# Queries and keys turned by two transposing DMAs instead of six TensorE transposes and two copies

## The chip, the cores and the metric

The kernel runs on one NeuronCore of a Trainium2 chip. Its engines each work through a list of instructions in order: TensorE (PE in the profile, with PEld for the loading of the stationary operand), VectorE (DVE), ScalarE (ACT), GpSimd (POOL) and SyncE (SP), which here issues all DMAs. The metric is the device time of one execution in microseconds; lower is better.

## The reference

One inference step of a single hybrid layer, for 1024 frames of a new stream and 32 frames of a running one (1056 rows, model width 1024). Cut to what matters here:

```python
z = rmsnorm(x, g) @ w_in                      # q,k,v of attention; q,k,v,gate of retention; two gates
qa = rmsnorm(qa.reshape(B, T, 8, 2, 64), g_q) # 8 heads, two maps of 64 each
ka = rmsnorm(ka.reshape(B, T, 8, 2, 64), g_k)
s  = einsum('bqhcd,bkhcd->bhcqk', qa, ka) * 64**-0.5    # chunk-causal mask, chunks of 64
p  = softmax(s);  a = p[:, :, 0] - lam * p[:, :, 1]
o_a = diff_out(einsum('bhqk,bkhe->bqhe', a, va))
o_r = ret_out(retention(qr, kr, vr), g_ret)   # chunkwise-recurrent, with decay
x = x + (sigmoid(gate_a) * o_a + sigmoid(gate_r) * o_r) @ w_o
x = x + (silu(h @ w_gate) * (h @ w_up)) @ w_down
x = x + sigmoid(rmsnorm(x) @ w_ple_gate) * (p_in @ w_ple)
```

The normalised keys and the values are outputs as well, as is the retention state.

## The kernel before

Inputs are float32. Each matmul operand is held as a float16 pair, high and low part, and a product is three float16 matmuls. The first part of the kernel, up to about 1040 us, does the projections, attention and retention; the second part does the output projection, the feed-forward block and the last gate. Only the first part is touched by the change.

The first part works on 72 units, (head h, tile i) for 8 heads and 9 tiles. Tiles i = 0 to 7 are 128 rows of the new stream; tile i = 8 is the 32 rows of the running stream, which is worked on as 128 partitions with 32 valid rows (R = 128, RT = 32). For each step, `project` makes one PSUM bank `pj` (128 x 512) for the A side of unit s (query, key, value, retention query and key; lines 734 to 736, or 745 for i = 8) and one for the B side of unit s - 4 (retention value and gates). Then:

- `unit_a` scales query and key into `z` (L1022), normalises them (L1036 to L1045), stores the key and the value as output (`kv`, L1048 on POOL and the DMA L1049), makes the float16 pairs of query and key in the tile `qst` (six groups of 128 columns: two for the query, four for the key; L1060 and L1061 on ACT, L1063 and L1064 on DVE), and turns them: six TensorE transposes (L1072) into one PSUM bank of the pool "o", then two copies through the helper at L388, one into `kT` (four groups, at the columns of this tile) and one into `q4` (two groups).
- `attend` computes scores from `q4` and `kT` (L875, L878; L877 adds the mask), the maxima (L885), the exponentials (L895), combines both maps (L909), turns the result (L924, L931 to L935), and multiplies by the values (L943 to L947).
- `unit_b` does the retention (L1142 to L1175), the gates, and the mix, which is turned (L1237) and stored to DRAM by a DMA (`mixT`, L1246).

`kT` has one buffer for a head (all tiles), `q4` and `qst` have two, `mixT` four; three PSUM banks serve the pool "o", one pair of banks the scores.

The order of the instructions on PE, DVE, ACT and POOL is written out by a planner, the class `Flow`, when the program is built. Each unit is a generator that yields what it needs: `M(us)` for PE, `V(n)` for DVE, `S(n)` for ACT, `G(n)` for POOL, `DM(mb)` for DMA (a resource "D"), `either(...)` for a choice, ("get", pool) and ("put", pool) for a buffer, ("wait", event), and ("delay", us). The planner starts whatever can start earliest by these costs (`LAT` = 0.13 us between dependent steps on different engines, `MARGIN` = 0.3 us ahead of a step of PE that follows another engine's), and the instruction is emitted at that moment. On the chip each engine then runs its list in order and waits where an input is not there yet. The DMAs on SP are not in the hand-written order of these four engines; they are queued in SP's own list. The loads of weights are L407, 1 MB each, for blocks that are used later.

Of the kernel before, what the change touches and what calls it, by code (L numbers as in the profile page):

```python
# [12 lines left out]
F16 = mybir.dt.float16  # L13
# [8 lines left out]
P = 128  # L22
D = 1024
# [35 lines left out]
def V(n, f=1.0, x=0.0):  # L59
    return {"V": 0.07 + x + f * n / 960.0}  # L60


def S(n, x=0.0):
    return {"S": 0.1 + x + n / 1200.0}


def G(n, x=0.0):
    return {"G": 0.15 + x + 0.0021 * n}


def M(us):
    return {"M": us}


def DM(mb):
    return {"D": mb * 2.9}


def either(*ds):
    out = {}  # L80
    for d in ds:
        out.update(d)
    return out
# [100 lines left out]
def kernel(  # L184
# [26 lines left out]
    nc = tc.nc  # L211
# [11 lines left out]
    def sm(n, tag, bufs=2, dt=F32):  # L223
        return small.tile([P, n], dt, tag=tag, name=tag, bufs=bufs)
# [162 lines left out]
    def copy(e, out, in_):  # L387
        (nc.scalar.copy if e == "S" else ENG[e].tensor_copy)(out, in_)  # L388
# [99 lines left out]
    with ExitStack() as pa:  # L488
# [3 lines left out]
        id16 = ca.tile([P, P], F16, name="id16")  # L492
# [24 lines left out]
        ps_o = pa.enter_context(DT(name="ps_o", bufs=3, space=PSUM))  # L517

        cs_sb = hp.tile([P, NT, 2, 32], F32, name="cs_sb")
        kT = hp.tile([P, 4, T], F16, name="kT")  # L520
# [227 lines left out]
        def fold(i, ps):  # L748

            if i < NT - 1:  # L750
                return ps, "pj"
            yield ("get", "su")
            yield S(P)
            su = wk.tile([P, 4, TS], F32, tag="su", name="su", bufs=1)
            psv = ps[:, 0:8 * TS].rearrange("p (g a c) -> p g a c", g=4, a=2)
            nc.scalar.copy(su, psv[:, :, 1])
            yield V(P)
            nc.vector.tensor_tensor(out=suz[:, :, 0:TS], in0=psv[:, :, 0], in1=su, op=ALU.add)
            yield M(0.5)
            for g in range(4):  # L760
                nc.tensor.transpose(out=ps[:, g * P:g * P + P], in_=suz[:, g], identity=id32)
            yield ("put", "su")
            return ps, "pj"

        def rms_small(ss, R, n, tag):

            yield G(0, 0.5 + 0.2 * n)
            r = sm(n, tag + "r", 6)
            nc.gpsimd.tensor_scalar(out=ss[0:R], in0=ss[0:R], scalar1=EPS, scalar2=None, op0=ALU.add)
            nc.gpsimd.tensor_tensor(out=r[0:R], in0=ss[0:R], in1=neghalf[0:R, 0:n], op=ALU.pow)  # L770
            return r
# [239 lines left out]
        def unit_a(h, i, ps, dA, e):  # L1011
            R, RT = P, P if i < NT - 1 else TS
            t0 = i * P
            yield ("wait", ("pa", h))
            if i == NT - 1:
                yield ("wait", ("cache", h))
            yield ("prio", -1)
            ps, buf = yield from fold(i, ps)
            yield ("get", "z")
            yield S(256, 0.05)  # L1020
            z = wk.tile([P, 2, P], F32, tag="z", name="z", bufs=3)
            nc.scalar.activation(z[0:R], ps[0:R, 0:256], AF.Copy, scale=dA[0][0:R])  # L1022
            yield ("get", "kv")
            kv = wk.tile([P, 2, P], F32, tag="kv", name="kv", bufs=3)
            if h * NT + i >= NQ:
                yield ("wait", ("ret",) + divmod(h * NT + i - NQ, NT))
            yield ("get", "rot")
            zr = wk.tile([P, P], F32, tag="zr", name="zr")
            flow.add(values(h, i, R, ps, kv, zr, dA, e, buf, (h, i)), 1)
            yield ("prio", 0)  # L1030

            zg = z.rearrange("p a (b c) -> p (a b) c", b=2)
            yield ("get", "sqz")
            yield S(256)
            sq = wk.tile([P, 4, 64], F32, tag="sqz", name="sqz")
            nc.scalar.activation(sq[0:R], zg[0:R], AF.Square, scale=0.125)  # L1036
            yield V(256)
            ss = sm(4, "qss", 6)
            nc.vector.tensor_reduce(out=ss[0:R], in_=sq[0:R], axis=AX.X, op=ALU.add)
            yield ("put", "sqz")  # L1040
            r = yield from rms_small(ss, R, 4, "qk")
            g = yield either(G(256), V(256))
            ENG[g].tensor_tensor(out=zg[0:R], in0=zg[0:R], in1=r[0:R].unsqueeze(2).broadcast_to([R, 4, 64]), op=ALU.mult)
            g = yield either(G(256), V(256))
            ENG[g].tensor_tensor(out=z[0:R], in0=z[0:R], in1=gqk[0:R], op=ALU.mult)  # L1045
            yield ("wait", ("v", h, i))
            yield G(128)
            nc.gpsimd.tensor_tensor(out=kv[0:R, 0], in0=z[0:R, 1], in1=kun[0:R].broadcast_to([R, P]), op=ALU.mult)  # L1048
            nc.sync.dma_start(out=kvo[h, t0:t0 + RT], in_=kv[0:RT])  # L1049
            yield ("later", ("kv", 3.0))  # L1050
            if i == NT - 1:
                yield V(P, 0.5)
                nc.vector.tensor_scalar(out=z[0:R, 1], in0=z[0:R, 1], scalar1=e["kre"][0:R], scalar2=None, op0=ALU.mult)

            yield ("get", "qst")
            yield S(384, 0.1)
            st = wk.tile([P, 6, 2, 64], F16, tag="qst", name="qst")
            zqk = z[0:R].rearrange("p a (m c) -> p a m c", m=2)
            sf = st[0:R].rearrange("p g a c -> p (g a) c")
            nc.scalar.copy(sf[:, 0:4:3], zqk[:, 0])  # L1060
            nc.scalar.copy(st[0:R, 2:4], zqk[:, 1].unsqueeze(2).broadcast_to([R, 2, 2, 64]))  # L1061
            yield V(384, 1.0, 0.07)
            nc.vector.tensor_tensor(out=sf[:, 1:3], in0=zqk[:, 0], in1=sf[:, 0:4:3], op=ALU.subtract)  # L1063
            nc.vector.tensor_tensor(out=st[0:R, 4:6], in0=zqk[:, 1].unsqueeze(2).broadcast_to([R, 2, 2, 64]),  # L1064
                                    in1=st[0:R, 2:4], op=ALU.subtract)
            yield ("put", "z")
            yield ("get", "o")
            yield M(0.336)
            pt = ps_o.tile([P, 1024], F16, tag="o", name="t")
            ptv = pt[:, 0:768].rearrange("p (g c) -> p g c", g=6)  # L1070
            for g in range(6):
                nc.tensor.transpose(out=ptv[:, g, 0:R], in_=st[0:R, g].rearrange("p a c -> p (a c)"), identity=id16[0:R, 0:R])  # L1072
            yield ("put", "qst")
            if h and i < NT - 1:
                yield ("wait", ("s", h - 1, NT - 2))
            g = yield either(V(512, 0.5), S(512, -0.09))
            copy(g, kT[:, :, t0:t0 + RT], ptv[:, 2:6, 0:RT])
            yield ("get", "q4")
            g = yield either(V(256, 0.5), S(256, -0.07))
            q4 = wk.tile([P, 2, P], F16, tag="q4", name="q4")  # L1080
            copy(g, q4[:, :, 0:R], ptv[:, 0:2, 0:R])
            yield ("put", "o")
            if i < NT - 1:

                if i:
                    yield ("wait", ("k", h, i - 1))
                yield ("set", ("k", h, i))
                NK = t0 + P
                sblocks = [(b0, min(512, NK - b0), kT[:, :, b0:min(b0 + 512, NK)]) for b0 in range(0, NK, 512)]
                yield from attend((h, i), i, R, q4, sblocks, True, [(P, vh[:, j, 0], vh[:, j, 1]) for j in range(i + 1)],  # L1090
                                  NK, scs, e["do_p"])
            else:
                sblocks = [(0, PAST, e["kcs"]), (PAST, TS, kT[:, :, t0:t0 + TS])]
                vblocks = [(P, e["vcs"][:, j, 0], e["vcs"][:, j, 1]) for j in range(4)]
                vblocks.append((P, vh[:, i, 0], vh[:, i, 1]))
                yield from attend((h, i), i, R, q4, sblocks, False, vblocks, PAST + TS, e["sc"], e["do_s"])
            yield ("put", "A")
            yield ("set", ("oa", h, i))
# [271 lines left out]
        def stream():  # L1370
# [10 lines left out]
            for s in range(NT * H + LAG):  # L1381
                at[0] = s
                h, i = divmod(s, NT)
                if h < H:
# [29 lines left out]
                    yield from project(wAs[h][0], ps, i, s)  # L1414
                    yield ("set", ("pA", s + 1))
                    flow.add(unit_a(h, i, ps, wAs[h][1], env[h]), 0)
                    if i == NT - 1:
                        yield ("put", "w")
# [670 lines left out]
```

## Time and profile before

| | |
|---|---|
| time, median of 3 runs | 1910.07 us (1909.86 to 1910.68) |
| span of the profiled execution | 1908.6 us |
| PE busy | 1859.8 us (97%) |
| DVE busy | 1497.7 us (78%) |
| ACT busy | 1087.3 us (57%) |
| POOL busy | 680.9 us (36%) |
| DMA | 146.90 MB, mean 77 GB/s |

The span is from the first to the last instruction of one execution under the profiler; nothing else of that execution is listed. An engine's busy time is the time in which at least one of its instructions runs. Matmuls overlap each other, so their listed durations add up to more than PE's busy time. In lists of groups, the middle number of three is the median duration in ns, and "xN" the number of instructions. A row "A <- B: t, n, m" in a list of waits says that A was idle for t us in total, n times, at most m us at once, until B ended. SPq is the queue of DMA issues on SP: the listed length is that of the issue, not of the transfer.

### The profile page before, as it was taken

How to read it: one execution, taken by the hardware profiler on the slowest of the kernel's cores; microseconds unless marked ns; L12 is line 12 of the kernel's file. 1: busy time of each engine (PE TensorE's matmuls, PEld its weight loads, DVE VectorE, ACT ScalarE, POOL GpSimd, SP SyncE). 2: the span in 40 equal slices, each digit the busy share in tenths (PEclk: the TensorE clock that was granted, in tenths of full speed). 3: DMA queues.
4: the chain of work that ended last, by engine and by line, in shares of the span. 5: the costliest groups of instructions: out<-in, count | busy, mean ns of one | idle time of the engine just before them, and what ended most of it. 6: DMA issues, size and time to landing. Idle time of an engine off the chain costs nothing.

```text
span 1908.6 us, 38365 instructions
## 1 busy us (share of the span) xinstructions
PE 1859.8 (97%) x14223; PEld 1220.3 (64%) x14223; DVE 1497.7 (78%) x3940; ACT 1087.3 (57%) x2842; POOL 680.9 (36%) x1149
## 2 busy tenths in 40 slices
PE   7999999999999999999999997999999999999999
PEld 3556565555655566655556685777777776666666
DVE  7888888788787787777887589999999986654364
ACT  7777677677676776766666345655555552101132
POOL 3654444445444544544442067333232300000010
PEclk9999999999999999999999999999999999999999
DMA  5222112112021121211215610222211116112031
GB/s 194 70 72 78 60 32 82 36 55 83 24 70 58 50 64 34 79 59 31 85 33 187 226 65 31 101 86 83 69 55 66 47 54 262 61 62 79 10 133 50
DMA packets 71949, 146.90 MB, mean 77 GB/s; under 512 B 25265, under 2 KB 52145, under 8 KB 63826
## 3 DMA queue, kind: packets, MB, share of 16 engines
q1 hardware_dynamic: 71762, 144.46, 22.7%
q8 instruction: 111, 1.82, 0.4%
q14 instruction: 76, 0.62, 0.1%
HBM read 113.09 MB, written 31.34 MB: 76 GB/s over the span
## 4 chain that ended last, share of the span: by engine, by line
PE 73%; DVE 12%; POOL 7%; ACT 5%; issue 2%; DMA 1%; SPq 0%; POOLq 0%; ACTq 0%; DVEq 0%
PE ps L474 10%; PE ps L475 10%; PE ps L476 10%; PE pj L734 7%; PE pj L736 7%; PE pj L735 7%; PE ps L1478 4%; PE ps L1477 4%; PE ps L1476 4%; ACT p L895 2%; DVE nm L885 2%; DVE w L467 1%; POOL qkr L770 1%; PE sc L875 1%; PE sc L878 1%
## 5 line engine op out<-in xcount | busy, mean ns | idle before, releaser
L734 PE MATMUL pj<-w,xh 128*128 128x512 f16 x1024 | 389.0, 380 | 2.8 <-ACT w L465 2.8
L735 PE MATMUL pj<-w,xh 128*128 128x512 f16 x1024 | 389.0, 380 | 0.6 <-DVE w L467 0.6
L736 PE MATMUL pj<-w,xh 128*128 128x512 f16 x1024 | 389.0, 380 | 0.0
L475 PE MATMUL ps<-mixs,w 128*128 128x352 f16 (+1 forms) x960 | 260.4, 276 | 5.9 <-DVE mixs L1501 5.9
L474 PE MATMUL ps<-mixs,w 128*128 128x352 f16 (+1 forms) x960 | 260.4, 276 | 0.3 <-ACT pws L1354 0.3
L476 PE MATMUL ps<-mixs,w 128*128 128x352 f16 (+1 forms) x960 | 260.5, 276 | 0.0
L476 PEld LDWEIGHTS <-w 128*128 128x128 f16 x1736 | 170.4, 98 | 56.2 <-issue 6.0
L474 PEld LDWEIGHTS <-w 128*128 128x128 f16 x1736 | 170.6, 98 | 54.4 <-issue 4.4
L475 PEld LDWEIGHTS <-w 128*128 128x128 f16 x1736 | 170.4, 98 | 49.8 <-issue 1.6
L736 PEld LDWEIGHTS <-xh 128*128 128x128 f16 x1024 | 100.3, 98 | 122.3 <-issue 1.9
L1634 POOL TENSOR_TENSOR st<-st 128x512 f32<-128x512 f32 x66 | 88.2, 1336 | 244.7 <-DVE w L1629 186.6
L734 PEld LDWEIGHTS <-xh 128*128 128x128 f16 x1024 | 101.3, 99 | 76.7 <-issue 3.7
L735 PEld LDWEIGHTS <-xh 128*128 128x128 f16 x1024 | 100.2, 98 | 74.6 <-issue 3.7
L895 ACT ACTIVATE p<-sc,nb,scs 128x256 f32<-128x256 f32 (+7 forms) x128 | 106.4, 832 | 71.5 <-POOL nb L887 49.0
L474 PE MATMUL ps<-tT,w 128*128 128x352 f16 (+1 forms) x528 | 144.0, 277 | 0.0
L475 PE MATMUL ps<-tT,w 128*128 128x352 f16 (+1 forms) x528 | 143.9, 277 | 0.0
L476 PE MATMUL ps<-tT,w 128*128 128x352 f16 (+1 forms) x528 | 143.8, 277 | 0.0
L1629 DVE SCALAR_TENSOR_TENSOR w<-st,gus,w 128x512 f16<-128x512 f32 x132 | 141.4, 1072 | 0.1
L885 DVE TENSOR_REDUCE nm<-sc 128x2 f32<-128x256 f32 (+6 forms) x112 | 102.7, 917 | 19.7 <-PE sc L878 18.4
L1478 PE MATMUL ps<-a,w 128*128 128x352 f16 x312 | 97.5, 313 | 0.5 <-DVE w L1720 0.5
L1477 PE MATMUL ps<-a,w 128*128 128x352 f16 x312 | 97.5, 313 | 0.0
L1476 PE MATMUL ps<-a,w 128*128 128x352 f16 x312 | 97.5, 313 | 0.0
(432 smaller groups left out, 4861.1 us busy)
## 6 DMA issues: line engine op xcount, KB each, us to landing
st<-in_win_dram SPq DMA_DIRECT2D x30, 1024.0 KB, 4.9
st<-in_wgu_dram SPq DMA_DIRECT2D x22, 1024.0 KB, 4.8
st<-in_wdn_dram SPq DMA_DIRECT2D x16, 704.0 KB, 4.7
out_dram<-kv SPq DMA_DIRECT2D x64, 128.0 KB, 1.7
a_d<-a SPq DMA_DIRECT2D x9, 528.0 KB, 2.6
b<-a_d SPq DMA_DIRECT2D x9, 528.0 KB, 7.5
mixs<-mix_d SPq DMA_DIRECT2D x8, 528.0 KB, 6.1
pw_d<-pws SPq DMA_DIRECT2D x12, 352.0 KB, 5.3
```

Of the source, the lines that this page charges most:

```text
L474: nc.tensor.matmul(out=ps, lhsT=wh, rhs=ah, start=first, stop=False)
L475: nc.tensor.matmul(out=ps, lhsT=wh, rhs=al, start=False, stop=False)
L476: nc.tensor.matmul(out=ps, lhsT=wl, rhs=ah, start=False, stop=last)
L734: nc.tensor.matmul(out=ps, lhsT=xhi, rhs=w[:, k, 0], start=(k == 0), stop=False)
L735: nc.tensor.matmul(out=ps, lhsT=xhi, rhs=w[:, k, 1], start=False, stop=False)
L736: nc.tensor.matmul(out=ps, lhsT=xh[:, k, 1, t0:t0 + P], rhs=w[:, k, 0], start=False, stop=(k == KD - 1))
L885: nc.vector.tensor_reduce(out=nm[0:R, mc], in_=pv, axis=AX.X, op=ALU.max, negate=True)
L895: nc.scalar.activation(pt[0:R, 0:NK], ps[0:R, p0:p0 + NK], AF.Exp, bias=nb[0:R, m:m + 1], scale=sc_ap[0:R], accum_out=Z[0:R, m:m + 1])
L1476: nc.tensor.matmul(out=ps, lhsT=wt[:, 0, j], rhs=a[:, 0, cs], start=(first and j == js[0]), stop=False)
L1477: nc.tensor.matmul(out=ps, lhsT=wt[:, 1, j], rhs=a[:, 0, cs], start=False, stop=False)
L1478: nc.tensor.matmul(out=ps, lhsT=wt[:, 2, j], rhs=a[:, 1, cs], start=False, stop=(last and j == js[-1]))
L1629: nc.vector.scalar_tensor_tensor(out=w[:, i, 1], in0=src, scalar=s, in1=w[:, i, 0], op0=ALU.mult, op1=ALU.subtract)
```

## The change

The six transposes, the PSUM bank and the two copies go. Two DMAs that transpose while they move are issued on SP: one turns the query's two groups of `qst` into `q4`, the other the key's four groups into the tile's columns of `kT`. Both read SBUF and write SBUF. The planner is told of them as time on its resource "D" and a delay until they have landed, and `qst` is given back after that delay.

```diff
+def X(us):
+    return {"D": us}
+
+
+def xbar(tiles):
+
+    return 0.5 + 0.027 * tiles
+
+
+def landed(tiles):
+
+    return ("delay", 2.0 + 0.03 * tiles)
...
             yield ("put", "z")
-            yield ("get", "o")
-            yield M(0.336)
-            pt = ps_o.tile([P, 1024], F16, tag="o", name="t")
-            ptv = pt[:, 0:768].rearrange("p (g c) -> p g c", g=6)
-            for g in range(6):
-                nc.tensor.transpose(out=ptv[:, g, 0:R], in_=st[0:R, g].rearrange("p a c -> p (a c)"), identity=id16[0:R, 0:R])
-            yield ("put", "qst")
             if h and i < NT - 1:
                 yield ("wait", ("s", h - 1, NT - 2))
-            g = yield either(V(512, 0.5), S(512, -0.09))
-            copy(g, kT[:, :, t0:t0 + RT], ptv[:, 2:6, 0:RT])
             yield ("get", "q4")
-            g = yield either(V(256, 0.5), S(256, -0.07))
+            rows = st[0:R].rearrange("p g a c -> p (g a c)")
             q4 = wk.tile([P, 2, P], F16, tag="q4", name="q4")
-            copy(g, q4[:, :, 0:R], ptv[:, 0:2, 0:R])
-            yield ("put", "o")
+            yield X(xbar(6 * RT // 16))
+            nc.sync.dma_start_transpose(out=q4[:, :, 0:R], in_=rows[:, 0:256])
+            nc.sync.dma_start_transpose(out=kT[:, :, t0:t0 + RT], in_=rows[0:RT, 256:768])
+            yield landed(6 * RT // 16)
+            yield ("put", "qst")
             if i < NT - 1:
```

## The prediction

> **What bounds the kernel now.** I read the page first (busy time, then the span in slices), then the stretch in which the change lies by windows, then the changed lines, then one unit in order of time, then the waits of the DMA queue.
>
> ```profile
> span 1908.6 us, 38365 instructions
> PE 1859.8 (97%) x14223; PEld 1220.3 (64%) x14223; DVE 1497.7 (78%) x3940; ACT 1087.3 (57%) x2842; POOL 680.9 (36%) x1149
> 40.00:1040.00 1000.00, 982.42 (x7273) 588.74 (x7272) 809.79 (x2475) 695.19 (x2063) 477.67 (x964) 1.00 0.20 62
> L1072 PE MATMUL t<-id,qst x432: 216/219/230, 41.9 to 998.7; 128*128 128x128 f16 x144
> ```
>
> The columns of the third line are the stretch, its length, and the busy time of PE, PE's weight load, DVE, ACT and POOL, then the granted clock, DMA share and GB/s. The 72 units of attention and retention run from about 40 to 1040 us; the 432 transposes to be removed lie in there. In these 1000 us PE is busy 982.42 and idle 17.6, while DVE has 190 us to spare and ACT 305, at the full clock. So PE is the bound here: work taken from PE shortens the stretch by what it costs in PE's stream, as long as nothing new makes PE wait. The remaining 870 us, the feed-forward part, are not touched.
>
> What PE waits for in the stretch is small: the whole list starts so (line, what ended the wait, us in total, times, longest).
>
> ```profile
> PE t L708 <- DVE w L698: 3.3, 2, 1.8
> PE t L1237 <- DVE aT L935: 2.0, 3, 0.7
> ...
> PE sc L875 <- ACT th L1198: 1.1, 3, 0.4
> PE sc L875 <- ACT p L895: 0.7, 3, 0.3
> ```
>
> The scores at L875, which read q4 and kT (named q and kT in the profile), hardly wait: the planner's order on PE puts them where their inputs are ready. That is the place to watch, since the change makes a DMA deliver both inputs.
>
> **The removed transposes.** One unit (head 4, i = 7) in order of time, start, length, engine:
>
> ```profile
> 612.50 0.41 DVE L1064 TENSOR_TENSOR qst<-z,qst 128x256 f16<-128x256 f32 x1
> ...
> 612.84 0.50 PE L1072 MATMUL t<-id,qst 128*128 128x128 f16 x6
> ...
> 613.17 1.03 PE L745 MATMUL pj<-xs,w 128*128 128x64 f16 x32
> ...
> 614.35 0.40 DVE L388 COPY kT<-t 128x512 f16<-128x512 f16 x1
> ...
> 614.80 0.28 DVE L388 COPY q<-t 128x256 f16<-128x256 f16 x1
> ...
> 615.14 0.39 PE L875 MATMUL sc<-kT,q 128*128 128x512 f16 x1 [0.36 <-ACT th L1198]
> ```
>
> The six transposes start at 612.84 and the next matmul at 613.17: they hold PE's stream for 0.33 us, 55 ns each, though each one is listed with 219 ns because matmuls overlap. 72 units x 0.33 = 23.8 us off PE. The weight loads that go with them lie in the same 0.33 us.
>
> **The removed copies.** They run on DVE and ACT:
>
> ```profile
> L388 DVE COPY kT<-t x57: 209/412/425, 52.4 to 989.9; 128x512 f16<-128x512 f16 x50, 128x128 f16<-128x128 f16 x7
> L388 DVE COPY q<-t x46: 269/280/292, 67.7 to 1000.2; 128x256 f16<-128x256 f16 x46
> L388 ACT COPY q<-t x26: 372/372/431, 47.2 to 990.7; 128x256 f16<-128x256 f16 x26
> L388 ACT COPY kT<-t x15: 265/585/623, 44.6 to 998.9; 128x512 f16<-128x512 f16 x14, 128x128 f16<-128x128 f16 x1
> ```
>
> DVE: 50 x 0.41 + 7 x 0.21 + 46 x 0.28 = 34.9 us; ACT: 14 x 0.585 + 0.27 + 26 x 0.372 = 18.1 us. Both engines have room, so I count nothing; at most it shortens chains that make up part of PE's 17.6 idle us (below, "more than forecast"). The bank of pool "o" that a unit held for transposes and copies comes free too: nothing for the same reason.
>
> **The added latency.** Today the scores start 615.14 - 612.91 = 2.23 us after qst is complete. The new chain is: SP wakes, issues the DMA for q4, then the one for kT, and the latter lands. No transposing DMA is in this trace, so I bound it by the plain ones that SP issues (issue lengths in ns min/median/max; then the landing times, KB each and median us from issue to landing):
>
> ```profile
> L1049 SPq DMA_DIRECT2D out_dram<-kv x72: 330/338/545, 42.4 to 995.7; - x72
> L798 SPq DMA_DIRECT2D st<-in_ckT_dram x8: 487/523/539, 102.2 to 893.7; - x8
> st<-in_win_dram SPq DMA_DIRECT2D x26, 1024.0 KB, 4.9
> out_dram<-kv SPq DMA_DIRECT2D x58, 128.0 KB, 1.7
> st<-in_ckT_dram SPq DMA_DIRECT2D x16, 256.0 KB, 3.7
> mix_d<-mixT SPq DMA_DIRECT2D x58, 64.0 KB, 2.0
> out_dram<-kv SPq DMA_DIRECT2D x8, 32.0 KB, 1.5
> ```
>
> q4 is 64 KB and kT 128 KB. Low end: one issue of 0.34 us, then the second lands 1.7 us after its own start: 2.0 us. High end: the two one after the other, each as slow as the slowest row of a like size, 3.7 us, behind issues of 0.52 us: 2 x (0.52 + 3.7) = 8.4 us. I take 4 us: the rows of the very sizes (1.7 and 2.0) are nearer to the low end, and a doubling is left for the turning.
>
> What counts is not this latency but how it compares with what the planner grants, because PE runs its list in order. From the new lines the planner charges X(0.5 + 0.027 x 48) = 1.80 us, a delay of 2.0 + 0.03 x 48 = 3.44 us, two hand-overs of 0.13 and the margin of 0.3 ahead of PE: 5.80 us from a complete qst to the scores. At 4 us the data is there 1.8 us early and PE never waits; the cover is this allowance together with the projection matmuls that the planner puts into the meantime. If the cover is gone, the price is the lateness itself, 72 times: each 0.1 us late in the mean costs 7.2 us, and 0.33 us late eats the gain.
>
> One unit in nine is granted less. For i = 8 the new lines use RT = 32: X(0.5 + 0.027 x 12) = 0.82, a delay of 2.36, with the rest 3.74 us, though the DMA for q4 still turns all 128 rows. At 4 us these eight units are 0.26 us late: 2 us in all, from nothing (at 2.0 us) to 8 x (8.4 - 3.74) = 37 us. I take 2 us.
>
> A unit holds its slot "A" 5.8 - 2.2 = 3.6 us longer. There are five such slots and a unit comes every 960 / 72 = 13.3 us, and the B side of a unit follows four steps later: no wait, cost nothing. The scores of a unit hold q4 (two slots) as now.
>
> **What is queued around the two DMAs on SP.** SP takes its list in order, and now two more per unit wait there for qst. Its waits and issues between 100 and 1000 us, and the issues around that unit:
>
> ```profile
> SPq L1049 <- POOL kv L1048: 254.8, 53, 7.3
> SPq L1246 <- DVE mixT L1244: 83.5, 20, 8.0
> ...
> SPq L407 <- DVE w L467: 36.4, 8, 8.9
> ...
> 611.20 0.34 SPq L1049 DMA_DIRECT2D out_dram<-kv  x1
> 616.93 0.52 SPq L1246 DMA_DIRECT2D mix_d<-mixT  x1
> ```
>
> Most of this waiting is an otherwise empty queue. In the unit above the store of kv (L1049) is issued 1.7 us before qst is complete and SP is then free until 616.93, so both DMAs go out at once. Behind them wait the store of mixT (four buffers, so nobody waits for it at a step of 13 us) and, if they fall there, the loads of weights at L407. The danger is the other order: the transposes behind a load that waits at the head of the queue for its buffer, 36.4 / 8 = 4.6 us in the mean. Eight such in 900 us, each with a chance of about a third that a unit's transposes fall behind it (4.6 of 13.3 us), make three units, late by up to 4.6 - 1.8 = 2.8 us: at most 8 us, at least nothing. I take 2 us. A load of 1 MB in flight (4.9 us, 26 of them) delays a later transpose on the same queue, but the planner books it on the same resource "D" for 2.9 us ahead of the transposes, so I take nothing for it, at most 26 x (4.9 - 2.9 - 1.8), 5 us.
>
> **Head starts.** kT has one buffer, so the first unit of a head may write it only after the last scores of the head before. That is a wait on SP, for PE:
>
> ```profile
> 500.46 0.38 PE L878 MATMUL sc<-kT,q 128*128 128x512 f16 x1
> 522.48 0.43 DVE L1064 TENSOR_TENSOR qst<-z,qst 128x256 f16<-128x256 f32 x1
> ```
>
> The last scores of head 3's i = 7 are at 500.46, head 4's first qst is complete at 522.91: 22 us apart, nothing. The first units, around 40 to 60 us, run while DVE and ACT are full; nothing either way.
>
> **Waits on PE.** The scores now wait for two DMA semaphores where they waited for copies. A separate semaphore instruction in PE's queue takes 51 ns:
>
> ```profile
> L1072 PEldq EVENT_SEMAPHORE  x2: 51/51/51, 119.7 to 943.2; - x2
> ```
>
> Between nothing and 72 x 2 x 0.051 = 7.3 us; with two such at 432 transposes it is rare, so I take 1 us.
>
> **Sum.** -23.8 (transposes) + 2 (units i = 8) + 2 (order on SP) + 1 (waits on PE) = -18.8 us: span 1908.6 -> 1889.8. The span of the profiled execution stands 1.5 us under the median of the unprofiled runs, 1910.07, so the runs should give 1891.3, 1.0% faster. A change of 0.2%, 3.8 us, is about what a measurement of this kernel can tell from none.
>
> **Rivals.**
> Slower, late by a little or more: the transposes land after their allowance. Place: L875, at the head of PE's list, with the projections queued behind. It decides from 5.80 + 0.33 = 6.13 us after qst. For it: the high end, 8.4 us, and that each lateness is paid by every unit, as the next unit's chain hangs on PE too. Against it: the low rows, and a queue that is idle at that moment. At the high end (8.4 - 5.8) x 64 + 37 = 203 us are lost, 1910 - 24 + 203 = 2089; half a microsecond past the allowance in all 72 gives 1910 - 24 + 36 = 1922. Chance 0.14.
> Slower, by far: the crossbar takes the six 128x128 blocks of a unit one after the other, each like a transfer of its own. A block is 32 KB, and the row of that size lands in 1.5 us: 6 x 1.5 = 9.0 us, late by 3.2 us in 64 units and 5.3 in eight, 247 us: 1910 - 24 + 247 = 2133. Against it: a plain DMA of 128 KB lands 0.2 us after one of 32 KB would (1.7 and 1.5), so plain ones do not work piece by piece. Chance 0.07. The Trainium skill speaks for this one: its page "VectorE: DVE Perf Modes", section The three transpose paths, gives a 128x128 bf16 block 390 ns on TensorE and 1309 ns by the DMA crossbar, which as an estimate from that page would be 7.9 us a unit and a time of about 2055. Its TensorE figure is not what a full stream shows here, 55 ns, so I give its other one little weight; and the skill's page "Advanced Engine Details and Errata", section X-Bar Transpose (TRN2), has such DMAs as fast as regular ones, by which the sum above would stand. No row of this trace shows one.
> No change: PE's gain is refilled by waits, about 0.3 us a unit, because the attention chain over DVE, POOL and ACT sets the pace once PE is lighter. For it: DVE is busy 81% of the stretch. Against it: the change takes 35 us from DVE too, and PE is idle 1.8% of the time. 1906 to 1914. Chance 0.09.
> Part of the gain: units next to loads and waiting stores on SP are late, all upper ends at once (8 + 5 + 7): 1910 - 24 + 20 = 1906; 1897 to 1906. Chance 0.17.
> More than forecast: half of PE's 17.6 idle us goes with the 53 us of copies: 1910 - 24 - 9 = 1877. Chance 0.08 (1875 to 1883).
> Forecast, 1883 to 1897: chance 0.45.
>
> **How the numbers follow.** Faster by over 0.2%: 0.45 + 0.08 + 0.17 = 0.70. Within: 0.09. Slower: 0.21. The range 1876 to 1918 holds all but the slower case beyond about 0.4%, some 0.8. The likeliest case's own range is 1883 to 1897.
>
> **What would show each step.** The end of the attention stretch some 19 us earlier and the part behind it as long as now. No L1072; L388 without kT and q. On SP two transposing issues a unit, starting within 0.5 us of the end of L1064; the kT one landing about 4 us behind it. PE's waits at L875 for a DMA under 5 us in total, most of them in the units i = 8. I am wrong if those waits come to over 24 us; if an issue holds SP for over 1 us, so that stores and loads pile up behind it; or if PE's idle time grows elsewhere (L924, L943, L1237), which would mean that the new order is worse and not the DMA.

## The result, and the profile after

| | before | after |
|---|---|---|
| time, median (lowest to highest of 4 runs) | 1910.2 us (1909.86 to 1910.68) | 1887.88 us (1885.31 to 1889.81) |
| after / before, with its 95% interval | | 0.9882 (0.987 to 0.9894) |
| PE busy / idle in the profiled span | 1859.8 / 48.8 us | 1838.3 / 49.4 us |

The change takes 22.3 us off; 1887.88 us is 3.4 us below the 1891.3 us predicted. The head of the page of after:

```profile
span 1887.7 us, 37668 instructions
PE 1838.3 (97%) x13791; PEld 1196.6 (63%) x13791; DVE 1487.0 (79%) x3874; ACT 1065.3 (56%) x2776; POOL 672.5 (36%) x1137
DMA packets 128780, 160.25 MB, mean 85 GB/s; under 512 B 82098, under 2 KB 108978, under 8 KB 120659
```

PE has lost 432 instructions and 21.5 us of busy time; its idle time is what it was. DVE's busy time fell by only 10.7 us: 103 of the removed copies were DVE's and 41 ACT's, but DVE has 66 instructions fewer and ACT 66 (x3940 to x3874, x2842 to x2776), since the planner, asked again, moved other work from ACT and POOL to DVE. The profiled run was 1889.55 us; the upper two of the four runs have a mean granted clock of 0.995, the lower two 0.998.

Where the time went is read from two landmarks: the last transpose of the mix, which ends attention, and the first and last matmul of the output projection behind it. Their rows (ns min/median/max, first and last start) in before,

```profile
L1237 PE MATMUL t<-cst_sb,mx x72: 272/273/329, 86.1 to 1043.1; 128*128 128x128 f32 x72
...
L474 PE MATMUL ps<-mixs,w x960: 236/309/355, 1053.8 to 1576.9; 128*128 128x352 f16 x96, 128*128 128x176 f16 x96
```

and in after:

```profile
L1245 PE MATMUL t<-cst_sb,mx x72: 272/273/329, 81.9 to 1018.2; 128*128 128x128 f32 x72
...
L488 PE MATMUL ps<-mixs,w x960: 236/311/501, 1030.9 to 1556.0; 128*128 128x352 f16 x96, 128*128 128x176 f16 x96
```

Attention ends 24.9 us earlier, the projection starts 22.9 us earlier and ends 20.9 us earlier, which is what the span shows (1908.6 - 1887.7). So 2.0 us are given back at the joint of the two and 2.0 us in the projection, some of whose matmuls now take 501 ns where the longest was 355: between 1031 and 1035 us they run at a granted clock of 0.50 (last section).

The new DMAs on SP, issue times in ns min/median/max; the first row of each pair is the issue, the second the landing. The query's, L1087:

```profile
L1087 SPq DMA_TRANSPOSE q<-qst x72: 1167/1195/2177, 43.1 to 978.0; - x72
...
DMA to landing us min/median/max: 2.3/2.3/5.0
```

and the key's, L1088:

```profile
L1088 SPq DMA_TRANSPOSE kT<-qst x72: 1170/1216/2066, 44.5 to 979.3; - x72
...
DMA to landing us min/median/max: 2.3/2.4/4.2
```

One unit (head 4, i = 7) in order of time, with the same columns as in the prediction:

```profile
600.16 0.28 DVE L1077 TENSOR_TENSOR qst<-z,qst 128x128 f16<-128x128 f32 x1
...
600.36 0.41 DVE L1078 TENSOR_TENSOR qst<-z,qst 128x256 f16<-128x256 f32 x1
...
600.50 1.19 SPq L1087 DMA_TRANSPOSE q<-qst  x1
...
601.78 1.22 SPq L1088 DMA_TRANSPOSE kT<-qst  x1
...
603.09 0.55 SPq L1254 DMA_DIRECT2D mix_d<-mixT  x1
...
606.34 0.38 PE L889 MATMUL sc<-kT,q 128*128 128x512 f16 x1
```

The query's DMA starts even before qst is complete, since its columns come from L1077. It holds SP until 601.69; the key's starts 1.0 us after qst is complete (600.77) and, at 2.4 us to land, its data is there 3.4 us after qst. Over the 72 units, too, the key's DMA starts 1.0 us after qst in the median. The scores come 5.57 us after qst: 2.2 us of slack. PE's list of waits between 40 and 1000 us begins

```profile
PE t L722 <- DVE w L712: 3.5, 3, 1.8
PE t L1245 <- POOL mx L1240: 2.7, 5, 0.6
PE sc L889 <- ACT p L909: 1.9, 2, 1.5
PE t L1245 <- DVE mx L1240: 1.8, 4, 0.5
```

and has no row in which a DMA of the change is waited for.

### The profile page after: what moved, and what is told of

Its sections match the earlier page's. It is cut to its first block, busy times and chain, and to the rows that moved or that the text cites. A ratio compares the mean times of both kernels' runs of the same rounds, so it can differ in the third digit from the quotient of the medians.

```text
span 1887.7 us, 37668 instructions
## 1 busy us (share of the span) xinstructions
PE 1838.3 (97%) x13791; PEld 1196.6 (63%) x13791; DVE 1487.0 (79%) x3874; ACT 1065.3 (56%) x2776; POOL 672.5 (36%) x1137
## 2 busy tenths in 40 slices
DMA packets 128780, 160.25 MB, mean 85 GB/s; under 512 B 82098, under 2 KB 108978, under 8 KB 120659
## 4 chain that ended last, share of the span: by engine, by line
PE 72%; DVE 14%; POOL 6%; ACT 4%; issue 3%; DMA 1%; SPq 0%; POOLq 0%; DVEq 0%; ACTq 0%
PE ps L488 9%; PE ps L489 9%; PE ps L490 9%; PE pj L748 7%; PE pj L750 7%; PE pj L749 7%; PE ps L1486 4%; PE ps L1484 4%; PE ps L1485 4%; PE t L938 1%; PE sc L889 1%; PE sc L892 1%; ACT p L909 1%; PE pj L759 1%; DVE w L1637 1%
## 5 line engine op out<-in xcount | busy, mean ns | idle before, releaser
L899 DVE TENSOR_REDUCE nm<-sc 128x1 f32<-128x640 f32 (+6 forms) x112 | 102.8, 918 | 15.5 <-PE sc L892 14.4
```

The costliest lines, as they stand in the source:

```text
L899: nc.vector.tensor_reduce(out=nm[0:R, mc], in_=pv, axis=AX.X, op=ALU.max, negate=True)
```

## The experiments

The total was right; what had to be tested is the split: the prediction gave the whole gain to PE's stream (-23.8 us), nothing to the copies, and +5 us to the DMAs. The kernel before read 1909.8 to 1910.6 us beside all of these runs.

**The old work put back, planner told.** First the transposes alone, into a bank of "o" that nobody reads, with everything else as after:

```diff
+            yield ("get", "o")
+            yield M(0.336)
+            ...
+            for g in range(6):
+                nc.tensor.transpose(out=ptv[:, g, 0:R], in_=st[0:R, g]..., identity=...)
+            yield ("put", "o")
             if h and i < NT - 1:
```

> The changed kernel, with the six TensorE transposes of each unit put back into a PSUM bank that nobody reads; the two DMAs still deliver q4 and kT, no copies. Theory (PE's stream sets the time of the attention stretch): the 72 x 0.33 = 24 us come back, 1888 -> 1908 to 1914, the time of before. Rival (the gain came from the copies taken off DVE and ACT, or from a better order): the time stays near 1888, at most 1895.

Measured 1902.42 us (1900.94 to 1902.67), ratio to before 0.9957 (0.9942 to 0.9972): 14.5 us over after. Less than the 24 us of stream, more than the rival allows. Then the two copies too, from that bank into a tile that nobody reads:

```diff
+            g = yield either(V(512, 0.5), S(512, -0.09))
+            copy(g, jk[:, 2:6, 0:RT], ptv[:, 2:6, 0:RT])
+            g = yield either(V(256, 0.5), S(256, -0.07))
+            copy(g, jk[:, 0:2, 0:R], ptv[:, 0:2, 0:R])
```

> As the run with the transposes put back, and the two copies per unit put back as well, from the bank into a tile that nobody reads (35 us on DVE or 18 on ACT); the DMAs still deliver. Theory (DVE and ACT have room): within 4 us of the run with the transposes alone, 1908 to 1916. Rival (the copies are part of the price): slower than it by 10 us or more, 1920 to 1945, since DVE then has all its old work and the DMAs' latency is on top.

1917.34 us (1914.99 to 1919.96), ratio 1.0039 (1.0027 to 1.0052): the copies cost 14.9 us, as much as the transposes. That is the rival's "10 us or more", though its range of 1920 to 1945 us is missed by 2.7 us; "nothing" is out. (The copies alone, planner told, have no time of their own: the kernel written for that, with a float32 tile that nobody reads, needed more SBUF than there is.) With all the old work back, the kernel is 7.1 us slower than before: that is what the DMAs, the longer path and the new order cost together.

**The same with the order kept.** In both kernels the planner made a new order, which may by itself move the time. So the works were put back without telling the planner: six transposes of the identity into the scores' own bank just ahead of the scores,

```diff
+                if ms[0] == 0:
+                    for g in range(6):
+                        nc.tensor.transpose(out=ps.bitcast(F16)[:, g * P:g * P + P], in_=id16, identity=id16)
```

> The changed kernel with six float16 transposes of the identity put on PE ahead of the scores of each unit, into the scores' own bank, where the first scores overwrite them. The planner is not told of them, so every engine's order stays exactly that of the changed kernel; only PE's stream is longer by 72 x 0.33 us. Theory (PE's stream sets the time): 24 us slower than the changed kernel, 1908 to 1915. Rival (the 14.5 us that the first run with the transposes put back showed is the true price, the rest falls into PE's idle time): 1899 to 1905.

1905.78 us (1901.28 to 1907.31, 10 runs), ratio 0.9973 (0.9964 to 0.9982): 17.9 us, between the two expectations. And two copies of 128x256 on DVE behind qst, into a tile that nobody reads:

```diff
+            jk = wk.tile([P, 2, P], F16, tag="jk", name="jk", bufs=1)
+            for _ in range(2):
+                nc.vector.tensor_copy(jk[0:R], z[0:R])
```

> The changed kernel with two copies of 128x256 from float32 to float16 put on DVE behind the making of qst, into a tile that nobody reads, without telling the planner: the order of all engines stays, DVE has about 0.5 to 0.7 us more a unit, 35 to 50 us in all, like the copies of the kernel before. The prediction's view (copies cost nothing, DVE is 79% busy): 1885 to 1893. Rival (DVE's work sits in the chains that PE waits for, as the second run suggested): 1898 or more.

1907.17 us (1905.39 to 1910.92, 10 runs), ratio 0.9987 (0.9978 to 0.9997): 19.3 us, so the copies were not free. The row of the copies in this kernel:

```profile
L1082 DVE CAST jk<-z x144: 273/293/541, 42.1 to 999.0; 128x256 f16<-128x256 f32 x144
```

That is 144 x 0.293 = 42 us on DVE, against 34.9 us on DVE and 18.1 us on ACT that were removed; PE has nothing new to do. PE's waits between 40 and 1000 us in this kernel begin

```profile
PE t L1248 <- DVE mx L1243: 5.3, 4, 1.4
PE t L722 <- DVE w L712: 3.8, 3, 1.9
PE t L1248 <- POOL mx L1243: 2.4, 5, 0.5
PE pr L1166 <- DVE qT L402: 2.2, 5, 1.1
PE t L722 <- DVE xh L733: 2.0, 2, 1.1
```

L1248 is the line of the mix transposes (L1245 in after). The wait for DVE's mix has gone from 1.8 to 5.3 us, the one for xh at L722 from 0.9 to 2.0, the one for qT from 1.7 to 2.2; further down stand rows for DVE that after does not have, of 1.0 us and less each. All of them are in other places than the copies. Both works together, in the same order:

> Both extra works of the two kernels before in one, in the changed kernel's own order of all engines: a unit's six transposes again on TensorE, ahead of its first scores, and two copies of 128x256 on VectorE behind qst, with nobody reading either; the two transposing DMAs stay. The planner is not told of them. Alone they cost 17.9 us (1905.78) and 19.3 us (1907.17) over 1887.88. If the two removals are worth separate things, the costs add: 1887.9 + 17.9 + 19.3 = 1925, and 1921 to 1929 holds it. If they are two prices of one and the same chain of units, so that a unit that is held by one isn't held again by the other, the sum falls short: 1907 to 1916, and the kernel before, at 1910.2, is this state with copies in place of DMAs. If they get in each other's way (transposes that VectorE's lateness pushes together, with no idle time left on TensorE to fall into), more than the sum: above 1929.

1924.47 us (1921.16 to 1924.86, 5 runs), ratio 1.0069 (1.0055 to 1.0083): 36.6 us over after, where the two alone add up to 37.2. The costs are separate. In all three of these kernels the work stands where the planner made no room for it; the two re-planned kernels above, with 14.5 and 14.9 us, are the check on that. How they are separate is seen in the spans and PE's busy time of the three, in the order transposes, copies, both:

```profile
span 1903.1 us, 38514 instructions
...
PE 1857.5 (98%) x14223; PEld 1219.4 (64%) x14223; DVE 1488.1 (78%) x3874; ACT 1065.6 (56%) x2776; POOL 669.8 (35%) x1137
```

```profile
span 1906.7 us, 37818 instructions
...
PE 1844.8 (97%) x13791; PEld 1194.7 (63%) x13791; DVE 1518.8 (80%) x4018; ACT 1066.3 (56%) x2776; POOL 677.5 (36%) x1137
```

```profile
span 1922.7 us, 38660 instructions
...
PE 1867.7 (97%) x14223; PEld 1219.0 (63%) x14223; DVE 1519.8 (79%) x4018; ACT 1066.3 (55%) x2776; POOL 675.3 (35%) x1137
```

Span less busy time is PE's idle time:

| PE busy / idle, us | copies there | copies gone |
|---|---|---|
| transposes there | 1867.7 / 55.0 | 1857.5 / 45.6 |
| transposes gone | 1844.8 / 61.9 | 1838.3 / 49.4 (after) |

Down a column, taking the transposes out lowers PE's busy time by 19 to 23 us and gives 4 to 7 us back as idle time: PE, with less to do, waits for the others. Along a row, taking the copies out lowers the idle time by 9 to 13 us, and the busy time by 7 to 10 us although no instruction of PE goes (this part isn't broken down further; a matmul ahead of a gap is listed with its whole length, and each of the four spends 10 to 20 us at half the clock, as the last section shows, which blurs such figures by a few us). The change does both, so idle time stays as it was, and the bookkeeping of before and after looks as if PE's stream alone had paid.

**The DMAs by themselves.** The kernel before, with the two DMAs of a unit added, from qst into a tile that nobody reads, and no scores behind them:

```diff
+            rows = st[0:R].rearrange("p g a c -> p (g a c)")
+            jk = wk.tile([P, 6, P], F16, tag="jk", name="jk", bufs=1)
+            nc.sync.dma_start_transpose(out=jk[:, 0:2, 0:R], in_=rows[:, 0:256])
+            nc.sync.dma_start_transpose(out=jk[:, 2:6, 0:RT], in_=rows[0:RT, 256:768])
             yield ("put", "z")
```

> The kernel before, with the two transposing DMAs of a unit added, from qst into a tile that nobody reads; the transposes, the two copies, the planner's input and the order of TensorE, VectorE, ScalarE and GpSimd stay as before. It prices the DMAs by themselves: 144 issues of 1.2 us on SP, 57000 more packets, and qst held until they are read, but no latency ahead of the scores. With all the old work put back into the changed kernel the time was 1917.34 (planner told) and 1924.47 (its order kept), 7 and 14 us over the 1910.2 of the kernel before. If that price is the DMAs' own presence (SP's queue, memory ports, the clock's dips), this kernel shows it: 1916 to 1925. If it is the longer path from qst to the scores and the order that the planner makes of it, the DMAs are harmless here: 1908.5 to 1913.

1913.12 us (1911.29 to 1914.13, 11 runs), ratio 1.0014 (1.0005 to 1.0024): +3.35 us on the 1909.77 of before beside it, just above the range for harmless DMAs. Two rows of this kernel, of the joint behind attention:

```profile
L474 PE MATMUL ps<-mixs,w x960: 236/309/351, 1057.3 to 1580.4; 128*128 128x352 f16 x96, 128*128 128x176 f16 x96
```

```profile
PE mt L275 <- DVE wam L435: 2.7, 1, 2.7
```

and the second of them in before:

```profile
PE mt L275 <- DVE wam L435: 0.9, 1, 0.9
```

The projection starts 3.5 us later than in before (1053.8) and is as long; 1.8 of the 3.5 are PE's longer wait at L275. Right behind that wait, from 1051.4 to 1054.8 us, the granted clock is 0.50 (it is 1.00 at the joint in before), which takes up to 1.6 us more. 144 issues of 1.2 us on SP, added in the middle of a full order, cost PE very little.

**The allowance.** Three kernels differ from after in one number, the delay after which the planner takes the data as landed. With the prediction's arithmetic a full unit is granted 5.80 us from qst to the scores; these grant 3.76, 2.36 and 7.8 us (the eight units i = 8, granted 3.74 us in after, get 1.73, 1.38 and 2.74):

```diff
-    return ("delay", 2.0 + 0.03 * tiles)
+    return ("delay", 1.4 * tiles / 48.0)     # 3.76 us
+    return ("delay", 0.0)                    # 2.36 us
+    return ("delay", 5.44 * tiles / 48.0)    # 7.8 us
```

> The planner grants the DMAs 2.04 us less (delay of 1.4 us in place of 3.44 for a full unit): 3.76 us from a complete qst to the scores. In the changed kernel's trace the kT issue starts 1.0 us behind qst and lands 2.4 us later, so the data is there at 3.4 us. Theory (only lateness past the allowance costs): 1883 to 1893, no difference that can be measured. Rival (the latency itself lies on the path, so that a shorter plan gains): 5 us or more faster, below 1883.

> The planner grants no delay at all: 2.36 us from a complete qst to the scores, while the data is there at 3.4 us. Theory (PE runs its list in order, each unit pays its lateness in full): about 1.0 us late in 72 units, 72 us, 1945 to 1975, with PE waiting at the scores (L889) for the DMA. Rival (the lateness is absorbed, since the wait lets the other engines catch up and the next unit comes no later): at most 20 us, below 1910.

> The planner grants the DMAs 2.0 us more than the changed kernel does (7.8 us from a complete qst to the scores); nothing else differs. Theory (five slots and two q4 buffers cover the latency, so latency that is planned for costs nothing): 1884 to 1893. Rival (latency costs by itself, part of what the run with all old work put back lost against before): 1895 or more.

| granted | time, us | ratio to before |
|---|---|---|
| 2.36 us | 1979.66 (1976.04 to 1980.56) | 1.036 (1.0344 to 1.0375) |
| 3.76 us | 1898.12 (1896.34 to 1898.99) | 0.9935 (0.992 to 0.995) |
| 5.80 us (after) | 1887.88 | 0.9882 |
| 7.8 us | 1896.54 (1895.49 to 1897.33) | 0.993 (0.9913 to 0.9947) |

All three times lie above the range of their theory, by 3.5 to 5.1 us. PE's waits between 40 and 1000 us, at 3.76 us granted,

```profile
PE sc L889 <- DMA kT<-qst: 9.1, 21, 1.1
PE sc L889 <- DMA q<-qst: 3.7, 2, 2.0
```

and at 2.36:

```profile
PE sc L889 <- DMA kT<-qst: 63.6, 56, 3.7
PE sc L889 <- DMA q<-qst: 5.3, 6, 2.8
```

With 1 us too little (2.36 against 3.4) nearly every unit waits, and the time rises by 92 us, 1.27 us for each of 72; 68.9 of the 92 us are the waits in these two rows. Lateness is paid every time, as the prediction had it. At 3.76 the median unit is just in time and the late ones cost 10 us. At 7.8 PE and its weight loads wait 1.0 us in all for these DMAs, and yet 8.7 us are lost, as the rival (latency costs by itself) had it. The units' pace shows that it isn't lost in attention (the first step of a unit, z; first and last start), in after

```profile
L1036 ACT ACTIVATE z<-pj,A0d x72: 452/473/480, 32.8 to 967.5; 128x256 f32<-128x256 f32 x72
```

and with 7.8 us granted:

```profile
L1036 ACT ACTIVATE z<-pj,A0d x72: 455/474/500, 33.0 to 966.2; 128x256 f32<-128x256 f32 x72
```

The last unit starts even 1.3 us earlier; then, between 1000 and 1070 us, PE's waits are

```profile
PE mt L289 <- DVE wam L449: 5.0, 1, 5.0
PE pj L488 <- ACT pws L1362: 2.0, 1, 2.0
```

where after has

```profile
PE mt L289 <- DVE wam L449: 1.8, 1, 1.8
...
PE pj L488 <- DVE pws L1364: 0.2, 1, 0.2
```

A slightly different order at the joint to the output projection is worth some 5 us of waiting, and behind the longer wait the granted clock is 0.50 for 10.2 us instead of 6.8. So no difference between two re-planned kernels below about 9 us is evidence on the change itself; that figure rests on this one pair.

**More of the same.** Three further kernels take other transposes off PE. The mix, split into its two float16 parts as rows, turned by one DMA (72 transposes of f32 off PE, 72 x 0.11 = 8 us):

```diff
-            nc.tensor.transpose(out=pt[:, 0:P], in_=mx, identity=id32)
+            nc.scalar.activation(mb[:, 0], mx, AF.Copy, scale=smx)
+            ...
+            nc.sync.dma_start_transpose(out=mt[:, :, 0:RT], in_=mb[0:RT].rearrange("p a c -> p (a c)"))
```

> The changed kernel with the mix of each unit turned by a DMA too: it is scaled and split into two float16 parts as rows (the same two instructions, now from SBUF), turned by one transposing DMA into mixT, and stored as before; 72 float32 transposes on PE go, and with them a bank. Theory (PE's stream): 72 x 0.11 us = 8 us less, 1876 to 1884. Rival (a third issue of 1.2 us a unit holds SP, and the transposes of queries and keys come late): PE waits at the scores for the DMA, 1890 or more.

1895.11 us (1894.67 to 1896.69), ratio 0.9923 (0.9908 to 0.9937): 7 us slower than after. That is in the rival's range, but not by its mechanism: PE waits 0.6 us in all for the DMAs of queries and keys. Its last unit starts at 958.7 (the row of z; the waits of PE between 1000 and 1070 us behind it):

```profile
L1036 ACT ACTIVATE z<-pj,A0d x72: 452/474/485, 32.8 to 958.7; 128x256 f32<-128x256 f32 x72
```

```profile
PE mt L289 <- DVE wam L449: 7.2, 1, 7.2
PE pj L488 <- ACT pws L1361: 4.1, 1, 4.1
```

The units are 8.8 us faster, as PE's 8 us say, and the joint takes 9.3 us of it back (7.2 + 4.1, less 1.8 + 0.2). In the joint this kernel is also at a granted clock of 0.50 for 17 us, after for 6.8. The rest isn't located.

The attention weights, split as rows and turned by two DMAs a unit (328 transposes of f32 off PE, some 36 us):

```diff
-            for j0 in range(0, nb_, 4):
-                ...
-                    nc.tensor.transpose(out=pt[0:n, j - j0, 0:R], in_=pm[0][0:R, j * P:j * P + n], ...)
+            nc.scalar.activation(hi, pm[0][0:R, 0:W], AF.Copy, scale=lsc[0:R])        # or on VectorE
+            nc.vector.scalar_tensor_tensor(out=lo, in0=pm[0][0:R, 0:W], ..., in1=hi, ...)
+            nc.sync.dma_start_transpose(out=aT[:, 0, 0:nb_, 0:R], in_=hi)
+            nc.sync.dma_start_transpose(out=aT[:, 1, 0:nb_, 0:R], in_=lo)
```

> The changed kernel with the attention weights turned by DMAs: scaled and split into two float16 parts as rows, then two transposing DMAs a unit into aT; 328 float32 transposes on PE and the banks they use go. Theory (PE's stream sets the time and planned latency is free): 328 x 0.11 = 36 us less on PE, 1850 to 1865. Rival (SP and the latency become the bound: five issues a unit, transposes of up to 128 blocks' worth in the way of those for queries and keys): no gain or slower, 1888 to 1950, with PE waiting at L957 or at the scores for DMAs.

1871.17 us (1870.82 to 1873.74), ratio 0.9799 (0.9784 to 0.9813): the fastest kernel of this study, 16.7 us below after and 39 below before, between the two expectations. Less than half of PE's 36 us arrive, and up to 5 us of the 16.7 may be the clock: in the profiled runs this kernel spends 10 us at 0.50, after 20. PE's waits between 40 and 1000 us are now led by

```profile
PE t L722 <- DVE w L712: 9.3, 3, 6.1
PE por L1165 <- DVE inn L1163: 5.9, 10, 1.1
PE sc L889 <- ACT p L909: 4.1, 7, 1.3
```

DVE and ACT again. Both at once:

> Attention weights and mix both turned by DMAs, on top of the change: 400 more float32 transposes off PE, 44 us of its stream, and six transposing issues of 1.2 us a unit on SP, 7.2 of 13 us. Theory (PE's stream counts, SP has room, the joint to the output projection gives some back): 1858 to 1870. Rival (SP is now too full, and transposes wait for each other): slower than the run with the attention weights alone, above 1873, with PE waiting for DMAs at the scores or at L957.

1901.25 us (1899.89 to 1902.18), ratio 0.9952 (0.9935 to 0.9968): 30 us slower than the weights alone, as the rival had it. (The expectation speaks of six transposing issues a unit; there are five, 6 us of SP's 13.) PE's waits now have DMAs in them:

```profile
PE t L722 <- DVE w L712: 9.3, 3, 6.1
PE sc L889 <- DMA kT<-qst: 8.6, 6, 3.0
PE sc L889 <- ACT p L909: 7.0, 9, 1.4
...
PE po L955 <- DMA aT<-p: 5.0, 3, 2.8
```

PE waits up to 3.0 us at once for a DMA here, 15.7 us with the query's row (2.1) that stands further down; whether the issue or the landing was late isn't broken down. It is not all of the 30 us: rows of ACT and DVE grew as well, and this kernel spends 41 us at a granted clock of 0.50, the one with the weights alone 10 us, which is worth up to 15 us.

## Why the prediction was right in sum and wrong in its split

**The removed copies, "I count nothing": the step that failed.** They were worth 14.9 us (planner told) to 19.3 us (order kept, with work on DVE alone). The reason given, that DVE and ACT have room, holds for their busy share and not for the chains: each copy on DVE stands in DVE's list ahead of work that PE waits for elsewhere. (So the waits of PE read; the chains were not followed further.) One part of the price no run here can show, since nobody reads the copies that were put back: in before the weight loads of the scores wait 17 times, 5.1 us in all, for the copy of the query. The prediction's own figure, 17.6 us of idle PE, was taken as the most that could be won there; with PE's list shorter, more idle time would have come.

**The removed transposes, -23.8 us: right mechanism, too large.** They were worth 14.5 us (planner told) to 17.9 us (order kept). PE's busy time does fall by 19 to 23 us; 4 to 7 us come back as idle time. That is a piece of the rival "no change", whose mechanism, the chain over DVE, POOL and ACT, was there, and which the copies' removal paid for.

**The DMAs and the wait for them, +5 us: too small.** Their presence costs 3.4 us, and with the longer path from qst to the scores 7 us (planner told, 1917.34 against 1910.2). With the order of after kept, the same comparison gives 14 us, but then the work put back stands where no planner chose. The sum as the runs have it: -14.9 (copies) -14.5 (transposes) +7.1 = -22.3 us. It comes out by construction, as differences of four kernels, and each term is uncertain by the 9 us that a new order alone can make. That the forecast sum fits is luck: the transposes paid 9.3 us less than forecast, the copies 14.9 us more, the DMAs and the path cost 2.1 us more.

**The latency, 4 us: right.** 3.4 us, with 5.80 granted. The two terms inside it were wrong in opposite ways: an issue is 1.2 us and not 0.34 to 0.52, and the DMA of the query starts before qst is complete. The 2 us for the units i = 8 and the 2 us for the order on SP did not show: PE waits for no DMA of the change at all. The warning sign "an issue holds SP for over 1 us" came true without its consequence in this kernel; in the one with five transposing issues a unit PE does wait for DMAs.

**Head starts, slots "A", waits on PE.** No row of after's waits names the first two. At the scores PE's queue has 18 semaphore instructions, 51 ns in the median, where before has 8: under 1 us, as counted.

**The rivals.** Late landing: its price was shown by a kernel that grants 2.36 us, its condition isn't met at 5.80. Part of the gain: no unit was late, so nothing was lost that way. Crossbar block by block: it needs 9 us a unit, and 3.4 were measured. The Trainium skill's 1309 ns a block (page "VectorE: DVE Perf Modes", section The three transpose paths), by the prediction's estimate 7.9 us for six, is not what this trace shows. "More than forecast" had the right cause, the copies, at half its size, and the wrong account of it: PE's idle time did not fall.

## What to carry to other kernels

A busy share does not say that work on a second engine is free: ask which of the bound engine's inputs stand behind it in that engine's list, and price it by putting the work back in an unchanged order. When an engine that is 97% busy loses work, count part of it as idle time to come, here a fifth to a third, unless the engines that feed it lose work too. Where a planner rewrites the order, vary one of its numbers to learn what a new order alone does before a small difference is read as an effect. And when a gap in the bound engine's stream grows, look at the granted clock behind it: here a wait of 1.8 us cost PE some 2 us more.

## What the hardware showed that was not expected

A transposing DMA holds SP for 1.2 us, two to four times as long as the plain ones (0.34 to 0.52), whether it moves 64 or 128 KB, and lands 2.3 and 2.4 us after the issue, so size hardly counts here; plain ones of these sizes, which go to DRAM, land in 2.0 and 1.7 us. The Trainium skill's page "Advanced Engine Details and Errata", section X-Bar Transpose (TRN2), has them as fast as regular ones: near enough for the landing, not for the issue.

The packets rose from 71949 to 128780, and the runs spread more, 4.5 us instead of 0.8. The clock has a part in that. One stretch in which it is lost, with the columns of the prediction's windows:

```profile
1000.00:1040.00 40.00, 37.13 (x271) 24.73 (x268) 28.59 (x91) 25.03 (x64) 4.87 (x11) 0.91 0.93 333
```

In narrower windows of the trace this 0.91 is 1.00 throughout but for 6.8 us at 0.50. While that lasts, matmuls of the projection follow each other every 0.29 us; behind it every 0.15. All such stretches of the two profiled runs (the last us of the kernel left out), with what went on in the 3.4 us ahead of each:

| kernel | granted clock 0.50, us | PE busy in the 3.4 us ahead | DMA share there |
|---|---|---|---|
| before | 1184.1 to 1190.9 | 0.00 | 0.01 |
| after | 69.6 to 73.0 | 1.57 | 0.13 |
| after | 1028.7 to 1035.6 | 1.47 | 1.02 |
| after | 1127.7 to 1131.1 | 0.91 | 0.17 |
| after | 1161.9 to 1168.7 | 0.56 | 0.00 |

So it is not the busy DMA engines that go with it (their share ahead is anything from 0.00 to 1.02) but idle time of PE. The traces of all 14 kernels, each cut from 20 us on into steps of 3.41 us that fit its first such stretch, have 58 drops to 0.50. All 43 full-clock steps in which PE is busy for 1.42 us or less are followed by one; of those with 1.43 to 2.12 us, 15 are and 56 are not; with more, none is. What decides in between, no run here tells. In after PE's wait of 1.8 us at L289 stands ahead of the second stretch, and 16 matmuls of the projection behind it took 0.29 instead of 0.15 us each, 2.2 us in all, the size of the 2.0 us that the projection gave back. In all, after spends 20 us at 0.50 and before 7, so up to 7 us of the gain were lost this way in the profiled run.
